# Weight tiles of 1024 columns moved and split whole in a hybrid conv, RG-LRU and RWKV-7 block

## The chip, the cores and the metric

The kernel runs on one core of a Trainium2 chip. A core has a matrix engine (TensorE; PE in the profile, PEld for its weight loads), VectorE (DVE), ScalarE (ACT), GpSimd (POOL) and SyncE (SP), each with an instruction queue of its own that is worked off in order. They share an on-chip memory of 128 partitions (SBUF); matmuls write to a second one (PSUM). DMA transfers bring data from the chip's main memory; those of this kernel are issued from the queues of SP, POOL and ACT. The engines wait for each other through semaphores.

The metric is device time in microseconds (us), the median of several timed executions. One more execution is recorded by the hardware profiler; all rows of the profile are of that one.

## The reference, cut to what matters

One layer over a sequence of 512 tokens of width 1024, in float32:

```python
h = rms_norm(x, norm1_g)
p = h @ w_in                                  # 1024 -> 3*1024 + 2*1024 + 3*1024 + 3*1024 + 256
y_a = b_a * causal_dwconv(c_a * x_a, conv_a_w)          # gated short convolution
y_b = rg_lru(causal_dwconv(x_b, ...), ...) * gelu(g_b)  # gated linear recurrence
y_c = rwkv7(...)                                        # state of 64x64 per head, 16 heads, chunks of 64
m = gate_a * y_a + gate_b * y_b + gate_c * y_c
x = x + m @ w_out                             # 1024 -> 1024
h2 = rms_norm(x, norm2_g)
x = x + square(relu(h2 @ mlp_w1)) @ mlp_w2    # 1024 -> 4096 -> 1024
return rms_norm(x, final_g)
```

## The kernel before

**Weights.** Every large weight matrix is laid out in main memory as tiles of 128 partitions by 1024 columns: 90 tiles of `w_in` (256 output columns for the low-rank inputs, `lr`, then `k`, `r`, `v`, and eight kinds for the two other mixers and the gates), 8 of `w_out`, which are read twice, 32 of `w1` and 32 of `w2`. That is 170 tile loads. For `w_in`, `w_out` and `w1` a tile holds eight blocks of 128 x 128, one for each of the eight blocks of the contraction; for `w2` it is 128 rows of the contraction by 1024 output columns.

**Split precision.** A float32 product is computed as three matmuls of type float32r. Each operand is split in two: `hi`, which is the value rounded to float32r, and `lo`, which is what is left. `mm3` (lines 155 to 158) issues hi*hi, hi*lo and lo*hi, in that order, into one accumulator. For a weight tile the rounding is a cast on ACT (line 134) and the remainder a subtraction on DVE (line 136, which the profile gives as line 97, where the helper `tt` stands).

**Loading a tile.** `load_half` (lines 130 to 137) loads 512 columns: a DMA on SP's queue into `raw`, the cast into `whi`, the subtraction into `wlo`. The three come from rings of buffers with 3, 4 and 4 halves. `load_w` does this for both halves of a tile. `wslice` picks the half and the 128 columns for one block of the contraction. One tile feeds 24 matmuls of 512 tokens.

**Stages.** First the input's norm and the `lr` projections (lines 202 to 339), whose weight halves are loaded between the pieces of the input, by hand. Then four groups of heads, each with `krv` (its k, r, v projections), `amat`, `inverse` (a triangular inverse: 31 steps of two dependent DVE operations, then a pair of transposes at line 502, another at line 507 and small matmuls), `chain` (the state carried through eight chunks) and `post`. The projections of the other two mixers (`ab`) and of the next group's `krv` fill PE meanwhile. Then the output projection `w_out` in two halves of 256 tokens, the first beside the last chain; then `mlp1` and `mlp2` and the final norm. In `mlp2` the weight is the moving operand: `mm3` takes 512 columns of `w2` for each of four blocks of tokens.

**What sets the order.** The program is traced in one order, and a planner then orders each engine's queue before the run, by its own estimates of durations: whenever an engine is free in its plan, the ready operation with the best priority goes next. Priority is the position in the trace, moved ahead by an offset where the code says so: loads of weights by `OFF` = 160, the chains of `inverse`, `chain` and the like by `CP` = 150, less inside some of them. An operation is ready in the plan when its inputs are there and, for one that fills a ring, when a buffer has been left by its last reader. `weave` (lines 742 to 753) traces steps of the groups and of the filling projections in turn, in a given ratio; `fill_main` (lines 761 to 780) traces `ab` alone until a group's inverse is done, then `krv` of the next group and `ab` alternately, a quarter of a projection at a time. On the chip the queues keep the planned order, whatever the real durations are.

**Memory.** Of each partition the weight rings take 3 x 2 KB, 4 x 2 KB and 4 x 2 KB. [...]

Of the kernel before, what the change touches and what calls it, by code (L numbers as in the profile page):

```python
# [9 lines left out]
F32 = mybir.dt.float32  # L10
F32R = mybir.dt.float32r
# [7 lines left out]
P = 128  # L19
# [10 lines left out]
S = 512  # L30
D = 1024
# [32 lines left out]
def chunk_plan():  # L64
    cols, names = [], {}

    def add(name, c):
        names[name] = len(cols)
        cols.append(c)

    nat = lambda base, j: base + np.arange(128) + 128 * j
    per = lambda base, q: base + perm_q(q)
    add(("lr", 0), C_LR + np.arange(128))
    add(("lr", 1), C_LR + 128 + np.arange(128))
    for g in range(NG):
        for jj in range(2):
            add(("k", 2 * g + jj), nat(C_K, 2 * g + jj))
            add(("r", 2 * g + jj), nat(C_R, 2 * g + jj))
        for h in range(2):
            add(("v", 2 * g + h), per(C_V, 2 * g + h))  # L80
    for q in range(8):
        for nm, base in (("c", C_C), ("x", C_X), ("b", C_B), ("ga", C_GA), ("xb", C_XB),
                         ("gb", C_GB), ("gatb", C_GA + 1024), ("gc", C_GA + 2048)):
            add((nm, q), per(base, q))
    return cols, names


COLS, CN = chunk_plan()
# [3 lines left out]
def block_kernel(ctx, tc, xt, win, par, mulr, sw, wout, w1, w2, fg, cst, eyes, out):  # L92
    nc = tc.nc
    v, ac, gp, pe, sy = nc.vector, nc.scalar, nc.gpsimd, nc.tensor, nc.sync

    def tt(o, a, b, op):
        return v.tensor_tensor(out=o, in0=a, in1=b, op=op)  # L97

    def stt(o, a, s, b, op0, op1):
        return v.scalar_tensor_tensor(out=o, in0=a, scalar=s, in1=b, op0=op0, op1=op1)  # L100
# [4 lines left out]
    MUL, ADD, SUB, MAX = ALU.mult, ALU.add, ALU.subtract, ALU.max  # L105

    def f(t):
        return t.bitcast(F32)

    cp = ctx.enter_context(tc.tile_pool(name="cp", bufs=1))  # L110
    wp = ctx.enter_context(tc.tile_pool(name="wp", bufs=2))
# [13 lines left out]

    def load_w(src):
        with tc.high_priority(offset=OFF):
            return load_w_(src)

    def load_half(src, i):  # L130
        raw = wp.tile([P, S], F32, tag="raw", name="raw", bufs=3)
        sy.dma_start(raw, src[:, i * S:(i + 1) * S])
        hi = wp.tile([P, S], F32R, tag="whi", name="whi", bufs=4)
        ac.copy(hi, raw)  # L134
        lo = wp.tile([P, S], F32R, tag="wlo", name="wlo", bufs=4)
        tt(lo, raw, f(hi), SUB)
        return hi, lo

    def load_w_(src):
        return [load_half(src, i) for i in range(2)]  # L140

    def wslice(w, kt):
        hi, lo = w[kt // 4]
        sl = slice((kt % 4) * P, (kt % 4 + 1) * P)
        return hi[:, sl], lo[:, sl]

    def split(pool, src, tag, rows=slice(0, P), bufs=None):
        th, tl = tag if type(tag) is tuple else (tag + "h", tag + "l")
# [6 lines left out]
    def mm3(ps, wh, wl, xh, xl, start=True, stop=True):  # L155
        pe.matmul(ps, wh, xh, start=start, stop=False)  # L156
        pe.matmul(ps, wh, xl, start=False, stop=False)  # L157
        pe.matmul(ps, wl, xh, start=False, stop=stop)  # L158
# [51 lines left out]
    gp.memset(ones, 1.0)  # L210
    n1t = pro.tile([P, KT], F32, name="n1t")
    ac.dma_start(n1t, par[:, PI["n1"]])
    wlr = [[load_half(win[CN[("lr", 0)]], 0)]]
    for a, n in ((0, 1), (1, 1), (2, 2)):
        sy.dma_start(xT[:, a:a + n], xt[a:a + n].rearrange("k p t -> p k t"))
    wlr[0].append(load_half(win[CN[("lr", 0)]], 1))
    for a, n in ((4, 2), (6, 2)):
        sy.dma_start(xT[:, a:a + n], xt[a:a + n].rearrange("k p t -> p k t"))
    wlr.append([load_half(win[CN[("lr", 1)]], i) for i in range(2)])
    gp.memset(epst[:, 0:1], EPS)  # L220
    wu = pc.tile([P, S], F32, tag="pu", name="wu")
    for i in range(NWARM):
# [6 lines left out]
    for kt in range(KT):  # L229
        sq = sp.tile([P, S], F32, tag=("v0", "v1", "bv0", "bv1")[kt % 4], name="sq", bufs=2)  # L230
        ac.activation(xgh(kt), xT[:, kt], AF.Copy, scale=n1t[:, kt:kt + 1])
        stt(xgl[:, kt], xT[:, kt], n1t[:, kt:kt + 1], f(xgh(kt)), MUL, SUB)
        with tc.high_priority(offset=OFFP):
            if kt % 2 == 0:
                gp.tensor_tensor(out=sq, in0=xT[:, kt], in1=xT[:, kt], op=MUL)
            else:
                ac.activation(sq, xT[:, kt], AF.Square)
                tt(sq, sq, sq_, ADD)
                pe.matmul(pst, ones, sq, start=kt == 1, stop=kt == KT - 1)
        mm3(t_lr0, *wslice(wlr[0], kt), xgh(kt), xgl[:, kt], start=kt == 0, stop=kt == KT - 1)  # L240
        sq_ = sq
# [19 lines left out]
    def proj_raw(w, t):  # L261
        for kt in range(KT):
            mm3(t, *wslice(w, kt), xgh(kt), xgl[:, kt], start=kt == 0, stop=kt == KT - 1)
# [7 lines left out]
    def proj(name):  # L271
        w = load_w(win[CN[name]])
        t = pp.tile([P, S], F32, tag="pp", name="pp")
        for kt in range(KT):
            wh, wl = wslice(w, kt)
            mm3(t, wh, wl, hh[:, kt], hl[:, kt], start=kt == 0, stop=kt == KT - 1)
            if kt % 2 == 1 and kt < KT - 1:
                yield
        return t
# [15 lines left out]
    def WP(tag, bufs=1):  # L295
        return pk.tile([P, S], F32, tag=tag, name=tag, bufs=bufs)
# [22 lines left out]
    lr = WP("ks")  # L319
# [579 lines left out]
    with tc.tile_pool(name="mw", bufs=2) as mw, \  # L899
# [12 lines left out]
        for fi in range(NF):  # L912
            t = pp.tile([P, S], F32, tag="pp", name="p1")
            w = load_w(w1[fi])
# [15 lines left out]
            ahi, alo = ahl(fi)  # L930
# [10 lines left out]
        with tc.tile_pool(name="fin", bufs=1, side="right") as fin:  # L941
            xr = fin.tile([P, 4, D], F32, name="xr2")
            gp.dma_start(xr, x2d.rearrange("i p d -> p i d"))
            fgt = fin.tile([P, D], F32, name="fgt")
            gp.dma_start(fgt, fg.to_broadcast([P, D]))
            bank = lambda pool, tag: pool.tile([P, S], F32, tag=tag, name="acc")
            acc = [[bank(pc, "pu"), bank(pc, "pS")], [bank(pc, "py"), bank(pm, "pm")],
                   [bank(pm, "pm"), bank(pp, "pp")], [bank(pp, "pp"), bank(pp, "pp")]]

            def mlp2(fi, w, i, h):  # L950
                ms = slice(i * P, (i + 1) * P)
                ahi, alo = ahl(fi)
                mm3(acc[i][h], ahi[:, ms], alo[:, ms], w[h][0], w[h][1],
                    start=fi == 0, stop=fi == NF - 1)

            for fi in range(NF - 2):
                w = load_w(w2[fi])
                for i in range(4):
                    for h in range(2):
                        mlp2(fi, w, i, h)  # L960
            wl2 = [load_w(w2[fi]) for fi in range(NF - 2, NF)]
            def last(i):
                ss = fin.tile([P, 2], F32, tag="fss", name="fss", bufs=2)
                x3f = xr[:, i] if i < 3 else fin.tile([P, D], F32, name="x3f")
                for h in range(2):
                    hs = slice(h * S, (h + 1) * S)
                    for d_ in range(2):
                        mlp2(NF - 2 + d_, wl2[d_], i, h)
                    stt(xr[:, i, hs], acc[i][h], sc2[:, i:i + 1], xr[:, i, hs], MUL, ADD)
                    junk = fin.tile([P, S], F32, tag="fj", name="fj", bufs=2)  # L970
                    ac.activation(junk, xr[:, i, hs], AF.Square, accum_out=ss[:, h:h + 1])
                    (v if (i, h) == (3, 0) else gp).tensor_tensor(out=x3f[:, hs], in0=xr[:, i, hs], in1=fgt[:, hs], op=MUL)
                sd = fin.tile([P, 2], F32, tag="fsd", name="fsd", bufs=2)
                tt(sd[:, 0:1], ss[:, 0:1], ss[:, 1:2], ADD)
                ac.activation(sd[:, 1:2], sd[:, 0:1], AF.Sqrt, bias=epst[:, 0:1], scale=1.0 / D)
                v.reciprocal(sd[:, 0:1], sd[:, 1:2])
                yield
                for h in range(2):
                    hs = slice(h * S, (h + 1) * S)
                    if h == 0 and i != 2:  # L980
                        ac.activation(x3f[:, hs], x3f[:, hs], AF.Copy, scale=sd[:, 0:1])
                    else:
                        v.tensor_scalar(out=x3f[:, hs], in0=x3f[:, hs], scalar1=sd[:, 0:1], scalar2=None, op0=MUL)
                    (ac if h == 0 and i != 2 else sy).dma_start(out[i, :, hs], x3f[:, hs])

            gens = [last(i) for i in range(4)]
            for i in (0, 1, 2, 0, 1, 3, 3, 2):
                next(gens[i], None)
# [75 lines left out]
```

## Time and profile before

| | before |
|---|---|
| median of 3 timed runs | 1141.97 us (1141.84 to 1142.87) |
| profiled execution | 1139.16 us |
| its span, first to last instruction | 1137.4 us |
| granted TensorE clock, mean | 0.985 |
| weight halves loaded, cast, split | 340 each |
| data moved by DMA | 114.69 MB, mean 101 GB/s |

How to read the rows that follow in the prediction. A group of instructions has its line, engine, operation, the names out<-in and the shape, the count, then busy time, the mean in ns of one, and the idle time of the engine just before, with what ended it. A row of waits says who waited, for whom, how long in total, how many times, and the longest. In an order of time each row has a start, a length, the instruction, and in brackets the idle time before it. A line such as L97 or L158 is a helper's, so that the names of the tiles tell what is meant: `wlo<-raw,whi` is the split of a weight, `pp` a projection, `p` mlp1, `acc` the output projection or mlp2.

### The profile page before, as it was taken

To read this page: it belongs to the slowest core of one execution; us is meant where nothing else is said; L and a number is where in the kernel's file an instruction comes from. 1 tells how busy PE (TensorE), PEld (TensorE's weight loads), DVE (VectorE), ACT (ScalarE), POOL (GpSimd) and SP (SyncE) were. 2 spreads that over 40 slices of the span, in tenths; PEclk is the share of its full clock that TensorE was granted. 3 is DMA by queue.
4 is the path that set the end of the run, shared out by engine and by line. 5 is a ranking of instruction groups with operands and counts; after the bars stand their busy time and mean duration, and the time that the engine had idled before them with its cause. 6 is when DMAs were issued, how large, how long until landed. Compare 5 with 4: busy or idle time off the path is not lost.

```text
span 1137.4 us, 17256 instructions
## 1 busy us (share of the span) xinstructions
PE 1102.8 (97%) x6396; PEld 867.8 (76%) x6396; DVE 786.2 (69%) x1537; ACT 549.1 (48%) x1005; POOL 58.9 (5%) x99
## 2 busy tenths in 40 slices
PE   8899989999999999999999999999999999999996
PEld 4677877778777778777777667898888888888885
DVE  7998996889976979976979957786444444222225
ACT  6655456534557534557534565565444443222224
POOL 3200000000000000000000020100000000000003
PEclk8899999999999999999999999999999999999998
DMA  5222222222332222332221262554322225322232
GB/s 190 76 95 63 85 83 71 71 93 68 95 112 76 76 93 68 101 107 75 75 89 65 84 195 75 176 188 160 96 94 94 93 93 178 107 95 93 93 102 93
DMA packets 61973, 114.69 MB, mean 101 GB/s; under 512 B 7232, under 2 KB 10816, under 8 KB 61888
## 3 DMA queue, kind: packets, MB, share of 16 engines
q1 hardware_dynamic: 54960, 95.49, 26.0%
q0 software_dynamic: 6352, 17.30, 4.7%
q8 instruction: 50, 0.82, 0.3%
q10 hardware_dynamic: 576, 0.79, 0.2%
q14 instruction: 35, 0.29, 0.1%
HBM read 104.64 MB, written 8.91 MB: 100 GB/s over the span
## 4 chain that ended last, share of the span: by engine, by line
PE 81%; DVE 14%; issue 3%; ACT 2%; DMA 0%; SPq 0%; DVEq 0%; ACTq 0%
PE pp L158 11%; PE pp L156 11%; PE pp L157 11%; PE acc L157 6%; PE acc L156 6%; PE acc L158 6%; PE p L158 5%; PE p L156 5%; PE p L157 5%; DVE wlo L97 3%; PE pA L461 2%; DVE Z L97 2%; DVE dg L97 2%; PE py L568 1%; DVE g L100 1%
## 5 line engine op out<-in xcount | busy, mean ns | idle before, releaser
L97 DVE TENSOR_TENSOR wlo<-raw,whi 128x512 fp32r<-128x512 f32 x340 | 235.8, 696 | 242.0 <-ACT whi L134 232.3
L134 ACT CAST whi<-raw 128x512 fp32r<-128x512 f32 x340 | 209.8, 619 | 364.3 <-PE acc L158 122.7
L158 PE MATMUL pp<-hh,wlo 128*128 128x512 f32 x696 | 284.0, 409 | 14.8 <-DVE wlo L97 14.7
L157 PE MATMUL pp<-hl,whi 128*128 128x512 f32 x696 | 281.5, 404 | 3.1 <-DVE hl L100 3.1
L156 PE MATMUL pp<-hh,whi 128*128 128x512 f32 x696 | 281.9, 406 | 1.3 <-ACT hh L257 1.3
L158 PEld LDWEIGHTS pp<-hh,wlo 128*128 128x128 f32 x696 | 132.6, 191 | 52.7 <-DVE wlo L97 21.7
L157 PEld LDWEIGHTS pp<-hl,whi 128*128 128x128 f32 x696 | 132.5, 190 | 34.1 <-DVE hl L100 3.7
L156 PEld LDWEIGHTS pp<-hh,whi 128*128 128x128 f32 x696 | 132.6, 190 | 32.8 <-ACT hh L257 1.8
L158 PE MATMUL p<-h2h,wlo 128*128 128x512 f32 (+1 forms) x264 | 103.0, 390 | 0.0
L156 PE MATMUL p<-h2h,whi 128*128 128x512 f32 (+1 forms) x264 | 102.9, 390 | 0.0
L157 PE MATMUL p<-h2l,whi 128*128 128x512 f32 (+1 forms) x264 | 102.8, 389 | 0.0
L157 PE MATMUL acc<-wlo,ah 128*128 128x512 f32 x256 | 99.7, 389 | 0.0
L156 PE MATMUL acc<-whi,ah 128*128 128x512 f32 x256 | 99.6, 389 | 0.0
L158 PE MATMUL acc<-whi,al 128*128 128x512 f32 x256 | 99.6, 389 | 0.0
L158 PEld LDWEIGHTS p<-h2h,wlo 128*128 128x128 f32 x264 | 49.7, 188 | 11.4
L157 PEld LDWEIGHTS p<-h2l,whi 128*128 128x128 f32 x264 | 49.7, 188 | 11.3
L156 PEld LDWEIGHTS p<-h2h,whi 128*128 128x128 f32 x264 | 49.7, 188 | 11.2
L157 PEld LDWEIGHTS acc<-wlo,ah 128*128 128x128 f32 x256 | 48.0, 188 | 10.1 <-DVE wlo L97 0.3
L156 PEld LDWEIGHTS acc<-whi,ah 128*128 128x128 f32 x256 | 48.0, 188 | 10.1
L158 PEld LDWEIGHTS acc<-whi,al 128*128 128x128 f32 x256 | 48.1, 188 | 10.0
L97 DVE TENSOR_TENSOR dg<-Z 64x31 f32<-64x31 f32 (+15 forms) x124 | 42.2, 340 | 4.1
L97 DVE TENSOR_TENSOR Z<-Z,dg 64x31 f32<-64x31 f32 (+15 forms) x124 | 42.2, 340 | 4.1
(299 smaller groups left out, 1525.4 us busy)
## 6 DMA issues: line engine op xcount, KB each, us to landing
raw<-in_win SPq DMA_DIRECT2D x180, 256.0 KB, 2.6
raw<-in_w SPq DMA_DIRECT2D x128, 256.0 KB, 2.6
raw<-in_wout SPq DMA_DIRECT2D x32, 256.0 KB, 2.6
swr<-in_sw SPq DMA_DIRECT2D x16, 128.0 KB, 2.2
x2T<-in_xt POOLq DMA_DIRECT2D x4, 512.0 KB, 6.3
x2d<-st POOLq DMA_DIRECT2D x8, 256.0 KB, 3.2
xr<-x2d POOLq DMA_DIRECT2D x1, 2048.0 KB, 8.9
xT<-in_xt SPq DMA_DIRECT2D x3, 512.0 KB, 6.1
```

Of the source, the lines that this page charges most:

```text
L97: return v.tensor_tensor(out=o, in0=a, in1=b, op=op)
L100: return v.scalar_tensor_tensor(out=o, in0=a, scalar=s, in1=b, op0=op0, op1=op1)
L134: ac.copy(hi, raw)
L156: pe.matmul(ps, wh, xh, start=start, stop=False)
L157: pe.matmul(ps, wh, xl, start=False, stop=False)
L158: pe.matmul(ps, wl, xh, start=False, stop=stop)
L461: pe.matmul(pts[h][:, ci], G_.BK[rows, jj, c], G_.AR[rows, jj, c], start=True, stop=True)
L568: mm = pe.matmul(py[64 * h:64 * h + 64, jj], w, x, start=first and jj == 0, stop=last, skip_group_check=True)
```

## The change

Whole tiles take the place of halves everywhere but for the first two tiles, whose halves are still moved and split one at a time, into whole tiles. A DMA moves 128 x 1024 values, the cast and the subtraction work on 1024 columns, and the rings hold two raw tiles, three `whi` and three `wlo`: 8, 12 and 12 KB of a partition. The matmuls are the same, in number and in operands' shape; they take their 128 or 512 columns from the wide tile. [...]

```diff
     def load_w(src):
         with tc.high_priority(offset=OFF):
-            return load_w_(src)
-
-    def load_half(src, i):
-        raw = wp.tile([P, S], F32, tag="raw", name="raw", bufs=3)
-        sy.dma_start(raw, src[:, i * S:(i + 1) * S])
-        hi = wp.tile([P, S], F32R, tag="whi", name="whi", bufs=4)
-        ac.copy(hi, raw)
-        lo = wp.tile([P, S], F32R, tag="wlo", name="wlo", bufs=4)
-        tt(lo, raw, f(hi), SUB)
-        return hi, lo
-
-    def load_w_(src):
-        return [load_half(src, i) for i in range(2)]
+            w = new_w()
+            sy.dma_start(w[0], src)
+            split_w(w, slice(0, D))
+            return w
+
+    def new_w():
+        return (wp.tile([P, D], F32, tag="raw", name="raw", bufs=2),
+                wp.tile([P, D], F32R, tag="whi", name="whi", bufs=3),
+                wp.tile([P, D], F32R, tag="wlo", name="wlo", bufs=3))
+
+    def split_w(w, sl):
+        raw, hi, lo = w
+        ac.copy(hi[:, sl], raw[:, sl])
+        tt(lo[:, sl], raw[:, sl], f(hi[:, sl]), SUB)
+
+    def load_half(w, src, i):
+        sl = slice(i * S, (i + 1) * S)
+        sy.dma_start(w[0][:, sl], src[:, sl])
+        split_w(w, sl)
 
     def wslice(w, kt):
-        hi, lo = w[kt // 4]
-        sl = slice((kt % 4) * P, (kt % 4 + 1) * P)
-        return hi[:, sl], lo[:, sl]
+        sl = slice(kt * P, (kt + 1) * P)
+        return w[1][:, sl], w[2][:, sl]
...
-    wlr = [[load_half(win[CN[("lr", 0)]], 0)]]
+    wlr = [new_w()]
+    load_half(wlr[0], win[CN[("lr", 0)]], 0)
...
-    wlr[0].append(load_half(win[CN[("lr", 0)]], 1))
+    load_half(wlr[0], win[CN[("lr", 0)]], 1)
...
-    wlr.append([load_half(win[CN[("lr", 1)]], i) for i in range(2)])
+    wlr.append(new_w())
+    for i in range(2):
+        load_half(wlr[1], win[CN[("lr", 1)]], i)
...
             def mlp2(fi, w, i, h):
...
-                mm3(acc[i][h], ahi[:, ms], alo[:, ms], w[h][0], w[h][1],
+                hs = slice(h * S, (h + 1) * S)
+                mm3(acc[i][h], ahi[:, ms], alo[:, ms], w[1][:, hs], w[2][:, hs],
...
-    nc = bacc.Bacc("TRN2", target_bir_lowering=False, num_devices=1)
+    nc = bacc.Bacc("TRN2", target_bir_lowering=False, num_devices=1, dynamic_dma_scratch_size=4096)
```

## The prediction, made before the changed kernel was run

> **What bounds the kernel now.** I read the page's first lines, then busy time by stretch, then who waited for whom, then DVE's and ACT's order of time where TensorE stood still.
>
> ```profile
> span 1137.4 us, 17256 instructions
> PE 1102.8 (97%) x6396; PEld 867.8 (76%) x6396; DVE 786.2 (69%) x1537; ACT 549.1 (48%) x1005; POOL 58.9 (5%) x99
> 780.00:953.00 173.00, 173.00 (x742) 139.12 (x741) 83.89 (x128) 74.00 (x128) 1.62 (x3) 1.00 0.30 99
> 953.00:1128.00 175.00, 174.87 (x771) 144.25 (x769) 50.90 (x76) 45.64 (x79) 7.84 (x7) 1.00 0.32 106
> ```
>
> In the stretch rows the columns after the length are busy time and count of PE, PEld, DVE, ACT and POOL, then granted clock, DMA share, GB/s. The two MLP stages (348 us) have no hole in PE: 173/742 is 0.233 us a matmul at full clock, 175/771 is 0.227. Nothing that arrives earlier there can help. A weight tile lasts PE 24 x 0.233 = 5.6 us, a half 2.8. A gain must come from before 780 us, and there from places where PE waits for a weight:
>
> ```profile
> PE pp L158 <- DVE wlo L97: 14.7, 11, 3.4
> PEld pp L158 <- DVE wlo L97: 21.7, 16, 3.8
> 109.00:166.00 57.00, 53.78 (x224) 42.86 (x223) 53.84 (x103) 24.14 (x39) 0.58 (x1) 0.97 0.25 79
> 289.00:318.00 29.00, 25.57 (x106) 19.09 (x105) 27.67 (x48) 13.28 (x20) 1.71 (x4) 1.00 0.33 100
> 456.00:490.00 34.00, 30.67 (x121) 23.16 (x121) 32.42 (x57) 14.47 (x23) 1.72 (x4) 0.95 0.32 97
> 628.00:661.00 33.00, 28.14 (x110) 21.18 (x109) 31.48 (x55) 14.39 (x22) 1.72 (x4) 0.95 0.30 97
> PEld pp L158 <- DVE wlo L97: 3.7, 1, 3.7
> PEld pp L158 <- DVE wlo L97: 5.6, 5, 3.1
> PEld pp L158 <- DVE wlo L97: 5.5, 5, 3.1
> PEld pp L158 <- DVE wlo L97: 6.9, 5, 3.8
> ```
>
> The first two rows are waits of the whole run (us in total, times, longest); the last four are the same wait inside the four stretches above them, in their order. They add up to 21.7: all of it lies in four stretches, one for each group's triangular inverse, and there DVE is busy 94 to 95% of the time. The matmul row gives 14.7, the weight-load row 21.7; the truth lies between (the second stall, shown below, puts 3.08 us between two matmul starts where 0.23 is normal: 2.85 lost, against 2.7 and 3.1 in the two readings). I take the middle, 18, shared out as the four rows stand: about 3.2, 4.6, 4.5 and 5.7. Three stretches also show a reduced clock: 0.03 x 57 + 0.05 x 34 + 0.05 x 33 = 5.1 us. So 23 us, 2% of the run, is all that late weights cost.
>
> Why DVE is late is seen in its order of time before the second stall:
>
> ```profile
> 303.17 0.69 DVE L97 TENSOR_TENSOR wlo<-raw,whi 128x512 fp32r<-128x512 f32 x1
> ...
> 308.25 0.69 DVE L97 TENSOR_TENSOR g<-g,u 128x512 f32<-128x512 f32 x1
> ...
> 309.72 0.69 DVE L97 TENSOR_TENSOR wlo<-raw,whi 128x512 fp32r<-128x512 f32 x1
> ...
> 311.41 4.04 DVE L502 STREAM_TRANSPOSE Z<-Z 32x1024 f32<-32x1024 f32 x2
> 315.48 0.69 DVE L97 TENSOR_TENSOR wlo<-raw,whi 128x512 fp32r<-128x512 f32 x1
> 304.13 0.62 ACT L134 CAST whi<-raw 128x512 fp32r<-128x512 f32 x1 [3.65 <-DMA raw<-in_win]
> 313.15 0.40 PE L157 MATMUL pp<-hl,whi 128*128 128x512 f32 x1
> 316.23 0.50 PE L158 MATMUL pp<-hh,wlo 128*128 128x512 f32 x1 [2.68 <-DVE wlo L97]
> ACT whi L134 <- PE pp L157: 112.2, 71, 6.8
> ```
>
> The split at 309.72 had its `whi` by 304.75 and stood behind work of the mixers (`g`), which has no raised priority. So the order was planned with that split not yet ready: with a ring of four halves it needs the buffer that PE leaves three halves earlier. The last row says the same from ACT's side: 71 casts waited for PE to leave a buffer. In the plan the splits therefore run about three halves (8.4 us) less cast and split (1.3) ahead of PE, 7.1 us; the real DVE is slower than the plan through an inverse, the two transposes of 4.04 us come last, and PE has caught up.
>
> **The change part by part.** Of 170 tiles 168 are loaded whole, two (the first) still by halves: 172 DMAs, casts and splits in place of 340 each.
>
> ```profile
> L97 DVE TENSOR_TENSOR wlo<-raw,whi 128x512 fp32r<-128x512 f32 x340 | 235.8, 696 | 242.0 <-ACT whi L134 232.3 <-PE pu L561 2.3 <-issue 0.2
> L134 ACT CAST whi<-raw 128x512 fp32r<-128x512 f32 x340 | 209.8, 619 | 364.3 <-PE acc L158 122.7 <-PE pp L157 112.2 <-PE p L157 74.4
> L97 DVE TENSOR_TENSOR Y<-Y,gst 128x1024 f32<-128x1024 f32 x6 | 7.3, 1222 | 0.1
> L524 ACT COPY AXt<-AR 64x1024 f32<-64x1024 f32 x8 | 8.4, 1044 | 2.2 <-PE pG L512 2.1
> ```
>
> *Durations.* DVE with 1024 columns: 1.22 us (bounds 1.22, this row, and 1.39, two of the old), so 0.17 less a tile, 28.6 us over the run. ACT with 1024: between 1.04 and 1.24; I take 1.06, the copy being nearest, so 0.18 less, 30 us. Both lie beside PE's work nearly everywhere and are worth nothing by themselves; only in the four stretches does DVE set the pace. Between 289 and 316 us nine halves are split, 4.5 tiles: 0.7 us less lateness per group, bounds 0 and 1.3 (eight tiles, the whole inverse).
>
> *Buffers.* Three whole tiles against four halves: the split of a tile can be planned once PE has left the tile three before it, 4 halves (11.2 us) ahead of the tile's first matmul and 14 ahead of its second half. Less cast and split of a whole tile (2.3) that is 8.9 and 11.7 against 7.1: 1.8 more at a tile's start, 4.6 at its middle. Three stalls fall at a tile's start, the last at a middle (counted by matmuls). Remaining: 3.2 - 1.8 - 0.7 = 0.7; 4.6 and 4.5 become 2.1 and 2.0; 5.7 - 4.6 - 0.7 = 0.4. That is 5.2 of 18, a **gain of 13**, bounds 0 (the order stays) and 18. What is late next is the same split after the transposes, by about 2 us.
>
> *Clock.*
>
> ```profile
> 628.00:652.00 24.00, 22.51 (x94) 17.08 (x93) 22.58 (x46) 11.38 (x18) 0.90 (x3) 1.00 0.27 88
> ```
>
> Ahead of its long stall the last stretch already waits 24.0 - 22.51 = 1.5 us in short pieces, at a clock of 1.00: the reduction follows the long stall alone, and what is left should bring none: **gain 5**, bounds 0 and 5.1. [...]
>
> *Longer operations in line.* A cast or split can't be interrupted. In the state chain, steps go from ACT and DVE to PE and back:
>
> ```profile
> PEld pu L561 <- ACT u L557: 10.5, 28, 0.6
> PEld pS L583 <- DVE sv L576: 7.2, 20, 0.4
> ```
>
> Splits take DVE for 1.22 of 5.6 us, 22%; what is left of one when a step arrives is 0.61 in place of 0.35 us on average: 0.06 a step. With 32 chunks of some five steps, 160 x 0.06 = 9 if all were exposed. The two rows have 48 exposed waits: **loss 3**, bounds 0 and 9.
>
> *DMA.* 512 KB a transfer, on SP's queue, two buffers:
>
> ```profile
> raw<-in_wout SPq DMA_DIRECT2D x11, 256.0 KB, 2.9
> swr<-in_sw SPq DMA_DIRECT2D x16, 128.0 KB, 2.2
> x2T<-in_xt POOLq DMA_DIRECT2D x4, 512.0 KB, 6.3
> raw<-in_w SPq DMA_DIRECT2D x128, 256.0 KB, 2.6
> 745.00:771.00 26.00, 25.88 (x217) 25.43 (x217) 20.82 (x46) 15.55 (x34) 2.21 (x4) 1.00 0.61 193
> ```
>
> From 128 to 256 KB landing grows by 0.4, so 512 KB is an estimate of 3.4 (2.6 + 2 x 0.4); four transfers of 512 KB together took 6.3, the upper bound. A raw buffer is held for landing, cast and split: 3.4 + 2.3 = 5.7, two of them give a tile every 2.9 us (4.3 at the upper bound). PE takes 5.6 in the projections and both MLP halves: covered even then. Only in the output projection (the last row, 26/217 x 24 = 2.9 us a tile) is it tight: **loss 1**, bounds 0 and 17 (16 tiles at 1.4 late, less a lead of two tiles).
>
> *At nothing.* At the start the `lr` halves are issued as before; the first whole tile, `k` 0, can be split earlier, but a split there can be slow:
>
> ```profile
> 29.73 1.75 DVE L97 TENSOR_TENSOR wlo<-raw,whi 128x512 fp32r<-128x512 f32 x1
> ```
>
> Twice this, 3.5, where a half stood now, is 1.75 more; less two halves (1.4) gone from before it: nothing, with bounds of -2 and 3. [...] mlp2 reads the same columns from a wider tile.
>
> Sum: -13 - 5 + 3 + 1 = -14. The profiled execution took 1139.16 us, span 1137.4 and 1.8 around it; 14 less is 1125. The median of the timed runs, 1141.97, is 2.8 above the profiled one, so the forecast is **1128**.
>
> **The rivals.** *A, the order stays.* If priorities and not buffers placed the splits, they stay behind the transposes; DVE saves 0.7 to 1.3 a group, and a tile's split ends 0.53 later than a half's. For: the transposes carry a priority raised by 150, close to the loads' 160. Against: the splits also stand behind work without any. Time: 1142 - 2 + 1 = 1141.
>
> *B, two raw buffers.* A transfer that must be whole before its cast can begin. If 512 KB lands later than 2 x 2.9 - 2.3 = 3.5 us, each tile of the output projection is late. For: 2.9 already for 256 KB in that stretch, DMA share 0.61. Against: two tiles of lead. At 6.3 it costs 17: 1128 - 1 + 17 = 1144, at 5 us (0.75 x 16 - 5.8 = 6) 1133; about 1139 between. [...]
>
> *C, slower: the whole split stands in the way.* As in A the order stays, and DVE's line now carries blocks of 1.22 us in the state chain. Each inverse's stall ends 0.53 later (+2), the one stretch at full clock gets its half clock as well (+1.7), and half to all of the 9 us of step delays is exposed (+4.5 to 9): +8 to 13, middle 1152. It decides from the point where no split of the next tile stands ahead of the transposes. For: DVE is 94% busy there, and the chain's steps were planned around pieces of 0.7. Against: shorter total work on both engines.
>
> **How the numbers follow.** Forecast 0.62, A 0.13, B 0.08, C 0.17. What a measurement of this kernel can tell from no change is about 0.2%, 2.3 us. Faster: 0.60 of the forecast, 0.03 of A, 0.02 of B, together 0.65. Same: 0.02 + 0.08 + 0.04 + 0.02 = 0.16. Slower: 0.02 + 0.02 + 0.15 = 0.19. The forecast's own range is 1117 (-23 from the stalls, -2 at the start) to 1139 (a gain of 8 in the stalls and none in the clock, less 4.5 in the steps and 1 in the output projection). The range for 8 in 10 adds A, most of B and the near edge of C: 1116 to 1150.
>
> **What would show it.** Right: 172 casts near 1.06 us and splits near 1.22; the weight-load wait on `wlo` at 4 to 8 us in place of 21.7; clock 1.00 in the stretches of the inverses; on DVE a split of the tile that PE takes next standing ahead of the pair of transposes. Wrong: a stall of over 3 us behind that pair (A or C); more than 9 us added to the waits of `pu`, `py` and `pS` (C); landing of `raw` over 3.5 us and PE below full in the output projection (B); or a new hole at the start, which I cost at nothing.

## The result, and the profile after

The changed kernel takes 1134.63 us (median of 6 runs, 1132.47 to 1135.17), the kernel before, run beside it, 1141.99 us (6 runs, 1137.2 to 1144.3). The ratio is 0.9935, 95% interval 0.9916 to 0.9954: 7.4 us faster. The forecast was 14 us faster, 1128, with a range of 1116 to 1150. So the sign and the range were right, and half of the gain is missing.

The profiled execution of the changed kernel took 1135.13 us, its span is 1133.3; that of before had 1137.4. This pair differs by 4.1 us, less than the medians do, and the readings of the two traces below are about those 4.1. The page after:

```profile
span 1133.3 us, 16256 instructions
...
PE 1103.6 (97%) x6396; PEld 871.2 (77%) x6396; DVE 767.6 (68%) x1369; ACT 520.1 (46%) x837; POOL 59.8 (5%) x99
...
L97 DVE TENSOR_TENSOR wlo<-raw,whi 128x1024 fp32r<-128x1024 f32 (+1 forms) x172 | 209.5, 1219 | 223.9 <-ACT whi L140 220.1
L140 ACT CAST whi<-raw 128x1024 fp32r<-128x1024 f32 (+1 forms) x172 | 178.9, 1040 | 296.9 <-PE acc L163 124.9
...
raw<-in_wout SPq DMA_DIRECT2D x16, 512.0 KB, 3.5
```

The change does what it says: 172 splits and 172 casts for 340, at 1.22 and 1.04 us, DVE 18.6 us and ACT 29.0 us less busy. PE's busy time, which ends the run, is the same within 0.8 us. The last row gives KB and the us from issue to landing: whole tiles land in 3.5 us.

TensorE's waits, from the view of who waited for whom (us in total, times, longest); lines after `mm3` have moved by 5 to 8, so `mm3` is now L161 to L163, the pair of transposes L510, the single one L515, the cast of `uh` L156:

```profile
PE pga L161 <- ACT uh L156: 4.6, 2, 2.3
...
PE pT L528 <- ACT dg L522: 3.1, 1, 3.1
PE pp L163 <- DVE wlo L97: 2.5, 1, 2.5
```

and those of the weight loads:

```profile
PEld pu L569 <- ACT u L565: 9.0, 25, 0.4
...
PEld pga L161 <- ACT uh L156: 5.5, 2, 2.8
...
PEld pp L163 <- DVE wlo L97: 3.9, 3, 2.9
...
PEld pS L591 <- DVE sv L584: 3.6, 11, 0.4
```

The wait for a late weight, 14.7 and 21.7 us in the two readings of before, is down to 2.5 and 3.9. But two rows are new. `pga` is a gate of the recurrent mixer, computed from `u`, which DVE makes and ACT casts; `pT` is one of the small products of the inverse, computed from ACT's copy of another product, `pG`, which takes what L515 transposes. Both go back to something that DVE makes. Four stretches around the inverses, somewhat longer than those of the prediction, first before, then after (length, then busy time and count of PE, PEld, DVE, ACT and POOL, then granted clock, DMA share, GB/s):

```profile
109.00:178.00 69.00, 65.78 (x377) 52.60 (x376) 62.27 (x115) 34.78 (x54) 1.22 (x3) 0.98 0.28 89
289.00:326.00 37.00, 33.57 (x140) 25.56 (x139) 33.86 (x57) 18.26 (x29) 1.71 (x4) 1.00 0.36 110
456.00:497.00 41.00, 37.67 (x151) 28.81 (x151) 37.03 (x64) 20.28 (x34) 1.72 (x4) 0.96 0.36 111
628.00:662.00 34.00, 29.14 (x115) 22.00 (x114) 32.37 (x56) 15.02 (x24) 1.72 (x4) 0.95 0.31 101
```

```profile
109.00:178.00 69.00, 65.90 (x393) 53.13 (x393) 60.01 (x102) 33.58 (x47) 1.22 (x3) 0.95 0.28 85
289.00:326.00 37.00, 34.44 (x139) 26.76 (x138) 32.65 (x50) 18.36 (x25) 1.72 (x4) 0.95 0.37 116
456.00:497.00 41.00, 38.45 (x156) 30.02 (x155) 36.59 (x57) 20.84 (x29) 1.73 (x4) 0.96 0.34 108
628.00:662.00 34.00, 31.50 (x155) 24.89 (x155) 31.87 (x51) 15.44 (x20) 1.72 (x4) 0.95 0.30 92
```

PE stood for 3.2 to 4.9 us in each before and still stands for 2.5 to 3.1, DVE is busy 87 to 94% of them, and the clock is reduced in all four, where before it was in three. What happened is seen in DVE's order of time in the second one:

```profile
308.00 2.12 DVE L510 STREAM_TRANSPOSE Z<-Z 32x1024 f32<-32x1024 f32 x1
310.15 1.23 DVE L97 TENSOR_TENSOR wlo<-raw,whi 128x1024 fp32r<-128x1024 f32 x1
311.41 2.06 DVE L510 STREAM_TRANSPOSE Z<-Z 32x1024 f32<-32x1024 f32 x1
...
314.10 0.75 DVE L100 SCALAR_TENSOR_TENSOR u<-u,part,u 128x511 f32<-128x511 f32 x1
314.76 1.23 DVE L515 STREAM_TRANSPOSE dg<-Z 32x1024 f32<-32x1024 f32 x1
315.92 0.70 DVE L100 SCALAR_TENSOR_TENSOR u<-u,part,u 128x510 f32<-128x510 f32 x1
316.55 1.20 DVE L97 TENSOR_TENSOR wlo<-raw,whi 128x1024 fp32r<-128x1024 f32 x1
317.68 0.73 DVE L100 SCALAR_TENSOR_TENSOR u<-u,part,u 128x509 f32<-128x509 f32 x1
```

and in PE's, a little later:

```profile
316.46 0.40 PE L163 MATMUL pp<-hh,wlo 128*128 128x512 f32 x1
319.16 0.50 PE L161 MATMUL pga<-uh,swbh 128*128 128x512 f32 x1 [2.30 <-ACT uh L156]
```

The split at 310.15 now stands between the two transposes, where before it stood behind them. The weight is there in time. PE runs on to the next thing that DVE owes it, the last step of `u` at 317.68, which the two transposes have made late as well, and stops there for 2.7 us, start to start, in place of 3.08.

In group 1 the last wait is for ACT. DVE had transposed `dg` by 160.5 us and PE had `pG` done by 164.5, but ACT copied it at 169.92 only, at the end of 7.7 us of work in line that had begun with a wait for DVE:

```profile
162.27 0.63 ACT L702 ACTIVATE u<-u 128x512 f32<-128x512 f32 x1 [1.74 <-DVE g L100]
...
167.81 2.10 ACT L532 COPY AXt<-AR 64x1024 f32<-64x1024 f32 x2
169.92 1.06 ACT L522 COPY dg<-pG 32x512 f32<-32x512 f32 x2
```

There DVE's lateness reaches PE through ACT's queue, and the order of that queue has a share in the stop that no run separates.

I call a **stop** two matmul starts over 0.9 us apart between 50 and 780 us (0.23 is normal). Before there are six, together 15.7 us, all for `wlo`. After there are four: 3.49 (`pT`, group 1), 2.70 and 2.71 (`pga`, groups 2 and 3) and 2.90 (`wlo`, group 4), together 11.8. The difference, 3.9 us, is most of the 4.9 by which PE's idle time fell (1137.4 - 1102.8 = 34.6 before, 1133.3 - 1103.6 = 29.7 after); PE's busy time grew by 0.8.

### The profile page after: what moved, and what is told of

Same layout as the page of the kernel before. It is cut to its first block, busy times and chain, and to the rows that moved or that the text cites. A ratio compares the mean times of both kernels' runs of the same rounds, so it can differ in the third digit from the quotient of the medians.

```text
span 1133.3 us, 16256 instructions
## 1 busy us (share of the span) xinstructions
PE 1103.6 (97%) x6396; PEld 871.2 (77%) x6396; DVE 767.6 (68%) x1369; ACT 520.1 (46%) x837; POOL 59.8 (5%) x99
## 4 chain that ended last, share of the span: by engine, by line
PE 75%; DVE 17%; issue 3%; ACT 2%; DMA 2%; SPq 0%; ACTq 0%; DVEq 0%
PE pp L161 10%; PE pp L162 10%; PE pp L163 10%; PE acc L162 6%; PE acc L163 6%; PE acc L161 6%; PE p L163 5%; PE p L161 5%; PE p L162 5%; DVE wlo L97 4%; DVE dg L97 2%; DVE Z L97 2%; PE pA L469 2%; PE py L576 1%; DVE u L100 1%
## 5 line engine op out<-in xcount | busy, mean ns | idle before, releaser
L97 DVE TENSOR_TENSOR wlo<-raw,whi 128x1024 fp32r<-128x1024 f32 (+1 forms) x172 | 209.5, 1219 | 223.9 <-ACT whi L140 220.1
L140 ACT CAST whi<-raw 128x1024 fp32r<-128x1024 f32 (+1 forms) x172 | 178.9, 1040 | 296.9 <-PE acc L163 124.9
L163 PE MATMUL pp<-hh,wlo 128*128 128x512 f32 x696 | 281.7, 406 | 2.5 <-DVE wlo L97 2.5
L161 PE MATMUL pp<-hh,whi 128*128 128x512 f32 x696 | 281.9, 406 | 0.6 <-DVE ks L100 0.3
L163 PEld LDWEIGHTS pp<-hh,wlo 128*128 128x128 f32 x696 | 132.4, 190 | 34.7 <-DVE wlo L97 3.9
L161 PEld LDWEIGHTS pp<-hh,whi 128*128 128x128 f32 x696 | 132.5, 191 | 32.8 <-DVE ks L100 0.8
L163 PE MATMUL p<-h2h,wlo 128*128 128x512 f32 (+1 forms) x264 | 102.9, 390 | 0.0
L161 PE MATMUL p<-h2h,whi 128*128 128x512 f32 (+1 forms) x264 | 102.9, 390 | 0.0
L161 PE MATMUL acc<-whi,ah 128*128 128x512 f32 x256 | 99.6, 389 | 0.0
L163 PE MATMUL acc<-whi,al 128*128 128x512 f32 x256 | 99.6, 389 | 0.0
L163 PEld LDWEIGHTS p<-h2h,wlo 128*128 128x128 f32 x264 | 49.7, 188 | 11.3
L161 PEld LDWEIGHTS p<-h2h,whi 128*128 128x128 f32 x264 | 49.7, 188 | 11.3
L161 PEld LDWEIGHTS acc<-whi,ah 128*128 128x128 f32 x256 | 48.0, 188 | 10.1
L163 PEld LDWEIGHTS acc<-whi,al 128*128 128x128 f32 x256 | 48.0, 188 | 9.8
```

The source lines that it names most:

```text
L140: ac.copy(hi[:, sl], raw[:, sl])
```

## The experiments

Theory T: in each inverse PE stops for as long as DVE is late around the transposes; the third tile only chooses which of DVE's products PE stops for, and a reduced clock comes on top. The rivals are named with each run. The number in brackets is the ratio to the kernel before, run beside it, with its 95% interval. A table of all the traces follows the list.

**The ring alone** (before, with six halves in place of four, and the changed kernel's scratch setting, `dynamic_dma_scratch_size=4096`).

```diff
-  hi = wp.tile([P, S], F32R, tag="whi", name="whi", bufs=4)
+  hi = wp.tile([P, S], F32R, tag="whi", name="whi", bufs=6)
-  lo = wp.tile([P, S], F32R, tag="wlo", name="wlo", bufs=4)
+  lo = wp.tile([P, S], F32R, tag="wlo", name="wlo", bufs=6)
```

> The kernel before, with halves as they were, but six whi and six wlo halves (as much memory as three whole tiles) and the smaller scratch. Theory (DVE's lateness): in the stretches of the inverses DVE is late by some microseconds whatever the ring; a deeper ring takes the wait from the weights' split (21.7 us of weight-load waits before, under 8 here) and hands most of it to the next thing that PE takes from DVE (u's split, pT); DVE keeps its 0.17 us a tile, so the time lies between the two kernels, 1136 to 1141. Rival (the ring alone makes the gain): as the changed kernel, 1133 to 1136. Rival (the fewer operations alone): as before, 1141 to 1143.

1149.26 us (1.0077, 1.0046 to 1.0108): slower than before, where 1136 to 1141 was expected. The waits of PE in that run:

```profile
PE pga L156 <- ACT uh L151: 8.0, 2, 4.0
PE pT L520 <- ACT dg L514: 5.5, 1, 5.5
...
PE pG L512 <- DVE dg L507: 1.8, 1, 1.8
```

The same memory as three whole tiles takes the weight waits away, as forecast, and the stops for `pga` and `pT` are longer than any of before. Earlier weights let PE run further ahead, so that it meets DVE's lateness in one piece: this fits the rows and was not tested by itself. In sum the stops grow by 1.2 us alone (table below). What grows more is the half clock, from 13.7 to 37.5 us, and the granted clock of the five executions is 0.975 to 0.981, below each of the 21 of before beside them (0.982 to 0.990). So most of the loss is the clock. The third tile by itself is a loss here.

**The width alone** (the changed kernel, with two `whi` and `wlo` tiles in place of three).

```diff
-  wp.tile([P, D], F32R, tag="whi", name="whi", bufs=3),
-  wp.tile([P, D], F32R, tag="wlo", name="wlo", bufs=3))
+  wp.tile([P, D], F32R, tag="whi", name="whi", bufs=2),
+  wp.tile([P, D], F32R, tag="wlo", name="wlo", bufs=2))
```

> The changed kernel with two whi and two wlo tiles in place of three. Theory: whole operations alone, with one tile of lead instead of two, bring the weight waits back, in the inverses and wherever two projections run side by side: 1145 or more, weight-load waits on wlo above 20 us. Rival (the gain comes from the fewer and wider operations): 1134 to 1138.

1149.01 us (1.0086, 1.0048 to 1.0124).

```profile
PE pp L163 <- DVE wlo L97: 19.4, 14, 3.7
```

With two tiles the weight waits are back, and larger than before. So neither half of the change gains by itself: the width without the ring is 0.9% slower than before, the ring without the width 0.8%, both together are 0.65% faster. With the ring of the same size, wide tiles (1134.63) beat halves (1149.26) here by 14.6 us; in the four stretches DVE is busy 87 to 94% of the time with wide tiles. Two things differ beside the width, though: the ring of `raw` (three halves there, two tiles here) and the order that the planner makes.

**The scratch alone** (before, with `dynamic_dma_scratch_size=4096` and nothing else changed).

```diff
-  nc = bacc.Bacc("TRN2", target_bir_lowering=False, num_devices=1)
+  nc = bacc.Bacc("TRN2", target_bir_lowering=False, num_devices=1, dynamic_dma_scratch_size=4096)
```

> [...] Every theory: no difference, 1140 to 1144. If it is faster by several microseconds, part of the change's gain is not the weights'.

1143.13 us (1.0013, 0.9992 to 1.0034): worth nothing, as expected.

**More DVE work** (the changed kernel, with one more transpose of 2 us in each inverse).

```diff
+  v.transpose(dg[32:64].rearrange("s l t -> s t l"), xt[0:32].rearrange("l s t -> l t s"))
   for b in range(2):
       v.transpose(TT[...]...
```

> The changed kernel with one more transpose of the same form (about 2 us of DVE) just ahead of the pair in each of the four inverses; its result is not used. Theory (DVE's lateness sets the stop): each 2 us of DVE ends the stop 2 us later, 6 to 9 us in all: 1141 to 1144. Rival (the stop is only a matter of what stands ahead of what, with slack behind it): under 2 us, 1134 to 1137.

1140.71 us (1.0000, 0.9979 to 1.0020), 6.1 more than the changed kernel and 0.3 below the theory's range.

```profile
PE pga L161 <- ACT uh L156: 9.1, 2, 4.5
PE pp L163 <- DVE wlo L97: 4.4, 1, 4.4
...
PE pG L521 <- DVE dg L516: 2.2, 1, 2.2
```

The three stops of groups 2 to 4 grow from 2.70, 2.71 and 2.90 to 4.94, 4.93 and 4.81 us: by 1.9 to 2.2 for the 2.08 added, one for one. Group 1 is an exception: its stop moved to `pG` and is shorter, 2.55 for 3.49.

**The transposes moved away from `u`** (the changed kernel; in groups 2 and 3 the second transpose of L510 and that of L515 stand some 20 DVE instructions later).

```diff
+  late = 4 if G_ in GS[1:3] else 0
+  for _ in range(late):
+      yield CPI
   for b in range(2):
-      v.transpose(TT[...]...)
-  for _ in range(NINV):
+      pin(late and b == 0, v.transpose(TT[...]...))
+  for _ in range(NINV - late):
```

> The changed kernel with the second transpose of the pair, and the one after it, put some ten DVE operations later in the second and third group, where PE needs their result more than 20 us later; the first and last group are as they were. Rival (placement: PE stops only because the pair stands ahead of u's convolution): the two waits of pga, 2.7 us each, and the half clock behind each go, 1126 to 1129. Theory (DVE is late as a whole and the next thing taken from it waits): the lateness is paid at the later place, 1132 to 1135.

1136.33 us (0.9972, 0.9955 to 0.9988), 1.7 more than the changed kernel and 1.3 above the theory's range.

```profile
PE pG L524 <- DVE dg L519: 4.6, 2, 2.3
```

The stop for `pga` is gone, and the same stop, 2.68 and 2.72 us, stands 18 to 20 us later at the inverse's own product. It goes with the transposes and not with `u`.

**Less DVE work** (the changed kernel with one transpose of 2 us less in each inverse; this leaves a part of the inverse filled with zeros).

```diff
-  for b in range(2):
+  gp.memset(TT[32:64, :, 32:64], 0.0)
+  for b in range(1):
       v.transpose(TT[...]...
```

> The changed kernel with one of the two transposes left out in each of the four inverses, its part of the result filled with zeros by POOL: 2 us less of DVE each. Theory (DVE's lateness, one for one): the four stops of 2.7 to 3.5 us shrink by 2 us each, and stops that short bring no half clock (4 x 1.7 us): 1134.6 - 8 - 7 = 1120, 1118 to 1124. Rival (cover or placement elsewhere): less than 4 us, 1131 or more. If the stops shrink and the half clock stays: 1127.

1117.71 us (0.9801, 0.9770 to 0.9831). Two of the four stretches:

```profile
289.00:326.00 37.00, 37.00 (x158) 29.27 (x157) 29.79 (x45) 20.31 (x28) 1.53 (x5) 1.00 0.39 122
456.00:497.00 41.00, 41.00 (x229) 32.62 (x228) 33.44 (x49) 22.81 (x31) 1.85 (x5) 1.00 0.40 129
```

PE has no hole left in these two and the full clock; no stop is left in any of the four. 2 us less of DVE's work in each inverse are worth 15.1 us against the changed kernel run beside it (next), and 4 x 2.06 = 8.2 explains only half of that. This is about what the stops and the clock behind them still cost, and how much the change left lying.

**The changed kernel once more**, beside the last run.

> The changed kernel once more, on the same chip as these two, as their base: 1132 to 1136 by every theory.

1132.82 us (0.9928, 0.9906 to 0.9950).

**Transposes that read, or write, in order.** If strides make them slow, DVE can be relieved honestly. First the copy that L510 reads is stored in the order of reading, then (the upper pair of lines) the one that L493 writes in the order of writing too. The step operations exchange their two axes.

```diff
-  v.transpose(la[32 * b:32 * b + 32].rearrange("l s t -> l t s"), ...)
+  v.transpose(la[32 * b:32 * b + 32], ...)
...
-                  xt[32 * b:32 * b + 32].rearrange("l s t -> l t s"))
+                  xt[32 * b:32 * b + 32])
```

> The changed kernel, with the inverse's transposed copy (the tile that the two transposes of L510 read) stored so that they read it contiguously. Theory: in the four inverses PE stops for as long as DVE is behind, and the two transposes of 2.06 us each are long because of their strides (the contiguous one of L515 takes 1.23 us). If only the reading side was strided they fall to 1.3 to 1.6 us, DVE gains 1 to 1.5 us an inverse, each stop of 2.7 us shrinks by that, and where it becomes short enough the half clock behind it (1.7 us) goes too: 1121 to 1131 us. Rival: the writing side or the number of rows sets their time, the transposes stay at 2.06 us and the time stays at 1132 to 1136 us; or the step operations, which now read and write the other stride, lose what the transposes gain, and the time is 1134 to 1140 us.

> As the run before, and the factor's copy stored in the same manner, so that the pair of transposes that L493 records at the head of each inverse writes contiguously too. Theory: as before, with up to 1.5 us an inverse more if that pair stands in DVE's way as well: 1117 to 1130 us. Rival: that pair runs where DVE is not behind, and the time is that of the run before within 2 us.

1132.92 us (0.9931, 0.9906 to 0.9956) and 1132.03 us (0.9928, 0.9900 to 0.9955): the same as the changed kernel. The groups of the first of these runs:

```profile
L493 DVE STREAM_TRANSPOSE Z<-AXt 32x1024 f32<-32x1024 f32 x8 | 16.6, 2075 | 0.2
L510 DVE STREAM_TRANSPOSE Z<-Z 32x1024 f32<-32x1024 f32 x8 | 16.1, 2006 | 0.3
L515 DVE STREAM_TRANSPOSE dg<-Z 32x1024 f32<-32x1024 f32 x4 | 4.9, 1225 | 0.0
```

Those of L510, reading in order, take 2.01 us. The same transposes, both sides out of order, take 2.08 in the changed kernel and 2.00 in the kernel before (L502), so reading in order takes nothing off that can be told from this, where 0.5 to 0.8 was expected; the rival held. In the second run L493, writing in order, takes 2.01 for 2.08. Why L515, of the same shape, takes 1.23 stays open: a transpose with both sides in order was not tried.

**Products moved to POOL** (the changed kernel; three products of 0.69 us for each of the eight blocks).

```diff
-  tt(g2, g2, gb, MUL)
+  gp.tensor_tensor(out=g2, in0=g2, in1=gb, op=MUL)
...
-  tt(u, u, ga, MUL)
+  gp.tensor_tensor(out=u, in0=u, in1=ga, op=MUL)
...
-  tt(cs, xs, cs, MUL)
+  gp.tensor_tensor(out=cs, in0=xs, in1=cs, op=MUL)
```

> The changed kernel, with three products of the gated recurrence and the short convolution (g2 times gb, u times ga, xs times cs, 0.69 us each on DVE, some of them in each inverse) moved to POOL, which is busy 5% of the span. Theory: what DVE sheds in an inverse shortens the stop by as much: 0.7 to 2.1 us an inverse and the half clock where the stop becomes short, 1121 to 1131 us. Rival: POOL and DVE slow each other. At the start of the run POOL's products of this size take 1.27 to 1.75 us, and DVE's splits beside them 2.30 in place of 1.23 us; then DVE gets back nothing, and the recurrence itself, whose steps wait for each other, is later: 1134 to 1142 us.

1135.63 us (0.9947, 0.9922 to 0.9973): no gain, the rival. POOL's order of time in that run:

```profile
289.73 1.82 POOL L714 TENSOR_TENSOR g<-g,g 128x512 f32<-128x512 f32 x1 [3.97 <-ACT g L713]
```

and DVE's at that time:

```profile
289.18 1.22 DVE L97 TENSOR_TENSOR wlo<-raw,whi 128x1024 fp32r<-128x1024 f32 x1
290.43 1.37 DVE L97 TENSOR_TENSOR dg<-Z 64x220 f32<-64x220 f32 x1
291.83 0.69 DVE L100 SCALAR_TENSOR_TENSOR u<-u,u 128x512 f32<-128x512 f32 x1
292.55 0.38 DVE L97 TENSOR_TENSOR Z<-Z,dg 64x220 f32<-64x220 f32 x1
```

The DVE operation that starts while POOL works takes 1.37 us; its sister right after takes 0.38, and the same operation of the changed kernel 0.38 too. It is so for all nine products of POOL in the inverses of groups 2 to 4: one DVE operation of 1.36 to 1.39 us each. So 0.69 moved off DVE costs another of its operations 1.0. Over the run 24 products of 0.69, 16.6 us, left DVE, whose busy time fell by 7.3 (767.6 to 760.3). What makes the one operation longer is not shown.

**Matmuls in the stops.** Is the reduced clock a price of its own, set by how long PE pauses? Extra matmuls of 0.233 us, into a tile that the next real one overwrites, shorten the pause and leave DVE's lateness as it is: first seven at each of the four stops, then eleven or twelve at three of them.

```diff
+  def awake(ps, n):
+      for _ in range(n):
+          pe.matmul(ps, hh[:, 0, 0:P], hh[:, 0], start=True, stop=True)
...
   pga = pm.tile([P, S], F32, tag="pm", name="pga")
+  awake(pga, 7 if q in (1, 3) else 0)
...
   t = pp.tile([P, S], F32, tag="pp", name="pp")
+  awake(t, 7 if name == ("gatb", 5) else 0)
...
   pg = pm.tile([P, 16, 32], F32, tag="pm", name="pT")
+  awake(pg.rearrange("p a b -> p (a b)"), 7 if G_ is GS[0] and half == 0 else 0)
```

In the second run the three numbers are 11, 12 and 0, since in group 1 the seven ran behind the stop and not in it.

> The changed kernel, with seven extra matmuls ahead of each of the four stops: ahead of the first one of pT in group 1, of pga for blocks 1 and 3 (groups 2 and 3) and of the projection of group 4 in which wlo is late. They multiply a block of hh by hh into the tile that the next real matmul overwrites, so the result is the same. Seven take 7 x 0.233 = 1.6 us, less than the stops (2.7 to 3.5 us), so DVE's lateness hides them. Theory: TensorE's half clock behind each stop follows from the length of its pause, and is a cost of its own beside the wait; with pauses of 1.1 to 1.9 us it goes in most of the four places and the time falls by 4 to 8 us against the changed kernel, to 1125 to 1130 us. Rival: the half clock follows from DVE's lateness or from the mean load over a longer time, not from the pause; then it stays, and the time is 1132 to 1136 us, or up to 1141 us if the extra matmuls themselves delay the real ones.

> As the run with seven extra matmuls a stop, with eleven ahead of pga in groups 2 and 3, twelve in group 4's late projection, and none in group 1, where the seven ran behind the stop and not in it. 11 x 0.233 = 2.6 us fill a stop of 2.7 us nearly whole; DVE's lateness stays as it is. Theory: pauses of 1.1 to 1.4 us, as the seven left them, are still long enough to bring the half clock in some executions, and pauses of some 0.3 us are not; the clock is then 0.992 or more in most executions and the time 1127 to 1131 us. Rival: the half clock doesn't hang on these three pauses; clock and time stay at the changed kernel's 0.985 to 0.989 and 1132 to 1136 us.

1136.04 us (0.9942, 0.9920 to 0.9963) with seven, 1132.29 us (0.9934, 0.9906 to 0.9962) with eleven: neither can be told from the changed kernel, and the theory missed its time twice. The stretches of groups 2 to 4 with eleven:

```profile
289.00:326.00 37.00, 36.77 (x157) 29.04 (x156) 32.88 (x50) 18.25 (x25) 1.71 (x4) 1.00 0.36 112
456.00:497.00 41.00, 40.77 (x173) 32.18 (x172) 35.49 (x56) 21.89 (x30) 1.72 (x4) 1.00 0.36 111
628.00:662.00 34.00, 33.26 (x196) 26.43 (x195) 31.09 (x47) 16.15 (x22) 1.72 (x4) 1.00 0.35 104
```

In the profiled execution the clock is full in these three places, as it was with seven, and the span is 1130.5. Over the timed executions the granted clock is 0.989 to 0.994 with eleven, mean 0.991, and 0.985 to 0.991, mean 0.987, in the 12 of the changed kernel; with seven it ranges from 0.985 to 0.994. So filling the pauses nearly whole does lift the clock, by 0.004, and what that is worth in time is not settled: 1132.29 stands beside 1134.63 and 1132.82, inside the intervals.

All traces side by side. Stops are start to start; half clock is the length of the records at 0.5 between 50 and 780 us. Under one of them matmuls of 512 columns start 0.43 us apart in place of 0.23 (changed kernel, 656.36 to 658.07 us), so some 45% of its length is lost while PE works; the sums below take half.

| kernel | stops, us | sum | half clock, us | span |
|---|---|---|---|---|
| before | 3.61, 3.08, 3.08, 1.15, 1.00, 3.77 | 15.7 | 13.7 | 1137.4 |
| before, scratch alone | 3.60, 3.06, 3.06, 1.15, 0.98, 3.76 | 15.6 | 20.5 | 1143.3 |
| changed | 3.49, 2.70, 2.71, 2.90 | 11.8 | 17.1 | 1133.3 |
| changed, once more | 3.47, 2.71, 2.71, 2.86 | 11.8 | 13.7 | 1130.9 |
| ring alone | 5.85, 4.38, 4.40, 2.22 | 16.9 | 37.5 | 1147.4 |
| width alone | ten, 1.02 to 4.12 | 21.7 | 10.2 | 1146.5 |
| one transpose more | 2.55, 4.94, 4.93, 4.81 | 17.2 | 27.3 | 1140.4 |
| transposes apart | 3.44, 2.68, 2.72, 2.93 | 11.8 | 30.7 | 1135.8 |
| one transpose less | none | 0 | 0 | 1114.7 |
| reading in order | 3.35, 2.64, 2.64, 2.81 | 11.4 | 13.7 | 1131.0 |
| reading and writing in order | 3.22, 2.65, 2.64, 2.67 | 11.2 | 13.7 | 1129.0 |
| products on POOL | 4.12, 2.43, 2.45, 2.47, 1.25 | 12.7 | 17.1 | 1133.9 |
| seven matmuls | 3.45, 1.10, 1.10, 1.42, 0.93 | 8.0 | 3.4 | 1129.9 |
| eleven matmuls | 3.44, 0.93 | 4.4 | 10.2 | 1130.5 |

Two traces of one kernel agree in the stops and not in the half clock: 17.1 and 13.7 us for the changed kernel, 13.7 and 20.5 for before without and with the scratch setting. So a difference of some 7 us in that column can be chance, and their spans differ by 2.4 and 5.9 us.

Against the first trace of the changed kernel, the sum of the stops and half of the half clock give +15.3 for the ring alone (spans: +14.1) and -20.4 for one transpose less (spans: -18.6). For the width alone they give 6.5 of 13.2; its other waits are single ones below 0.9 us. For the transposes apart they give 6.8 where the spans show 2.5, for one transpose more 10.5 where they show 7.1, and for before 2.2 where they show 4.1. So, the width alone aside, the count is good to some 5 us, and the half clock is not always worth half its length.

No version was found that computes the same and beats the changed kernel by more than the intervals.

## Why the prediction was right in sign and twice too large

**The weight wait: right.** It was to fall by 13 of 18. Measured as the forecast measured it, the middle of the two readings falls from 18.2 to 3.2, by 15; counted in stops, from 15.7 to 2.9, by 12.8. The lead of a third whole tile put the split ahead of the transposes in group 1 and between them in groups 2 and 3, as it was to show.

One row says less than the forecast took from it. The 112.2 us that casts waited for PE are of the whole run; between 289 and 326 us of before they waited little for PE and more for their transfers, which waited for DVE's splits to free `raw`:

```profile
ACT whi L134 <- DMA raw<-in_win: 5.7, 4, 3.6
ACT whi L134 <- PE pp L157: 0.8, 1, 0.8
SPq L132 <- DVE wlo L97: 22.2, 10, 5.3
```

So in that stretch DVE held up the loading of weights too. That the rings of `whi` and `wlo` are what removes the late weight is shown by the ring alone, which left `raw` at three halves.

**"What is late next": the step that failed.** The forecast said that the same split would be late by about 2 us, and took 13 us as gained. What is late next is another product that goes back to DVE: `u` in groups 2 and 3, where the stops are only 0.4 us shorter than before, and in group 1 ACT's copy of `pG`, behind work that had waited for DVE. That is 8.9 us of new stops, so that the stops lost 3.9 in all. Removing the wait for a late engine gained here only up to the next thing that came from that engine. That the lateness is what counts is shown by the runs with one transpose more and one less, that it moves by the run with the transposes apart, and that the ring alone gains nothing by the first run.

**The 0.7 us less lateness per group from shorter splits: right in kind, and probably the part that carries the change.** The width makes the difference between the ring alone (16.9 us of stops) and both (11.8): 5.1 us, 1.3 a group, the upper bound that the forecast gave for it. The ring of `raw` and the planned order changed along with the width, so how much of this is the width is not shown.

**The clock, 5: not seen in the profiles.** It needed the stops to go. Four of 2.7 to 3.5 us stayed, and the clock records show half clock behind each: 17.1 us of it after and 13.7 in the second trace, 13.7 and 20.5 before. The reading that it "follows the long stall alone" holds where the stops go (one transpose less, none), but not throughout: in the trace of before one piece of it, at 178.6 us, stands behind no stop, and none behind the stop at 313 us. In group 2 it followed a pause of 2.30 us, the one for `pga` that ended at 319.16 us: the record at 0.5 runs from 320.8 to 324.2. The medians differ by more than the profiled pair, 7.4 for 4.1. In 12 executions of before beside the last run the clock was 0.990 in four (1136.7 to 1137.5 us) and 0.981 to 0.985 in eight (1141.5 to 1145.9 us); in the six of the changed kernel it was 0.986 to 0.989. Some 6 us thus go with 0.007 of clock. Beside the changed kernel's repeat the mean clock was 0.9865 in 15 executions of before and 0.9873 in six of the changed kernel, at mean times of 1140.1 and 1132.8 us: by that slope, an estimate, the clock is worth less than 1 of these 7.3 us. Where the half clock lies in executions other than the profiled one was not seen, and how the medians' 7.4 share out stays open.

**The chain's steps, a loss of 3: not there.** The wait rows of `pu` and `pS` fall from 10.5 to 9.0 and from 7.2 to 3.6; other rows of these tiles rise, and all weight-load waits of `pu`, `py` and `pS` together stay at some 34 us. That a step of the chain stands behind a split is seen in before: the new `St` was done at 199.53 us, a split ran on DVE from 199.45 to 200.13, and DVE's copy of `St` began at 200.05.

**The output projection, a loss of 1: not there.** Whole tiles land in 3.5 us, against an estimate of 3.4, and from 712 to 771 us PE is busy for all but 0.3 us:

```profile
712.00:771.00 59.00, 58.67 (x551) 55.66 (x550) 45.26 (x96) 33.34 (x62) 2.25 (x5) 1.00 0.57 185
```

Rival B's point, 3.5 us, was just reached and two tiles of lead covered it.

**The start, at nothing:** it was not tried alone. The scratch setting, changed along with the tiles, is worth nothing by its own run (1.0013). Rival A holds in group 4 alone, where the split still stands behind the pair (stop 2.90 for 3.77); in the other groups something else than the weight is late. Rival C falls: the steps of the chain wait no longer than before.

How near the forecast came is in part luck. The two losses that did not come, 4 us together, hid a part of the miss: without them it would have been 18 us faster. And a range of 1116 to 1150 takes in the time of the kernel before, so that it held says little.

## What to carry to other kernels

When PE waits for a product of an engine that is busy 90% of a stretch, price the removal of that wait by the engine's lateness and not by the wait: look for the next product of the same engine that PE takes, and count only the time up to it. A deeper ring moves the stop and can make it longer (six halves: stops up to 5.85 us for 3.77, 0.8% slower than before); here it paid only together with wide operations, which take 0.17 us a tile off the late engine (1.22 for 1.39). To see what is left to gain, take a piece of the late engine's work out and time the rest: here 2 us an inverse were worth 15.

## What the runs showed of the hardware that was not expected

- Half clock of 3.4 us or more follows the stops of 2.7 to 3.5 us in all four places of the changed kernel's trace, and not the stop of 3.08 us at 313 us of before; stops that extra matmuls cut to 1.4 us or less were not followed by it in two profiled executions, and yet the timed median didn't move. Which pauses bring it, and why the mean clock of one kernel ranges from 0.981 to 0.990 between executions, stays open.
- A DVE operation on two operands in SBUF took 1.0 us longer (1.37 for 0.38 us) when it started while POOL multiplied, nine times out of nine in three inverses. Three that read `pA`, which matmuls write, kept their 0.69 us beside POOL's products at 97.7 and 103.4 us.
- Transposes of 32x1024 float32 on DVE take 2.00 to 2.08 us with one or both sides out of order, and 1.23 at L515, which writes in order and reads rows of 32 values in steps of 64.
